# Gate and up products with both halves of the activations in one 512-wide matmul, and the joins of a quad spread over its products

## The chip, the cores and the metric

The kernel runs on one core of one Trainium2 chip. The metric is the device time of one execution in microseconds (us), the median of three runs. The profile is of one further execution. TensorE (PE) multiplies, with its weight loads shown apart as PEld; VectorE (DVE) and ScalarE (ACT) do elementwise work; GpSimd (POOL) and SyncE (SP) here mostly issue DMAs. Each of them takes its instructions in the order of its own program and waits on semaphores for the others.

## The reference, cut to what matters

One encoder layer on 512 tokens of width 2048: a token mixer, a layer norm, and a SwiGLU block with `D_FF = 5632`. The change touches the first half of the last one:

```python
def swiglu(h, w_gate, w_up, w_down):
    return (jax.nn.silu(h @ w_gate) * (h @ w_up)) @ w_down
...
        h = x * (1.0 + sc_f) + sh_f
        y = swiglu(h, w_gate[l], w_up[l], w_down[l])
```

## The kernel before

**Three products for one.** Every fp32 operand is kept as a rounded part `hi` and a remainder `lo = x - hi`, and a product is `hi*hi + lo*hi + hi*lo` with three matmuls (helper `mm3`, lines 241 to 243 when `gu_product` calls it). Weights come by DMA as a `raw` tile of 128x1024; `split` makes `whi` on ACT (L276) and `wlo` on DVE (L277). Activations are the tiles `mhi`, `mlo`.

**Seven products for eight.** Gate and up are computed with a Strassen-like scheme on 2x2 blocks. The work is cut into 44 quads, numbered `n`: even ones are gate, odd ones up, and two that follow each other form a pair `p`. One quad has the seven products p1, q7, r6, p2, q5, q4, p3 (table `SEVEN`), each a contraction over 8 blocks of 128, so 8 x 3 = 24 matmuls, each 256 tokens wide. p1, p2, q5 and p3 multiply the activations themselves (`mhi`, `mlo`), q7, r6 and q4 sums of their blocks (tiles `R7`, `R6`, `R4`, which hold hi in their first 256 columns and lo in the next). Three PSUM banks collect a quad: `V` (p1, r6, q5, p3), `Y` (q7, q4) and `A` (p2).

**Sums of weight blocks.** Four of the seven products need sums of weight blocks: S3 for q7, S1 for q5, S2 for r6, S4 for p3. From the fifth quad on, DVE makes them from the raw blocks (`add_behind`: L1284, L1287, L1290, L1293, each 128x1024). For the first four quads (`NPRE = 4`) they were made earlier by DMAs.

**What sets the order.** One loop walks over all products; a step is one product. In step `s` the program first issues the split of the weights of step `s + 3` (`prepare`, with four `whi`/`wlo` pairs in turn, `NW = 4`), then the DMAs (`fetch_behind`), then the matmuls of the step, then what is done with its PSUM bank (`gu_use`), then the sums of weight blocks (`add_behind`, at steps given by a table of how many steps ahead). No scheduler reorders anything: on each engine the instructions stand in that order. In `gu_use` ACT copies banks out (`e`, `yv`, `vq`) and DVE joins them; a gate quad ends in Silu on ACT, an up quad in multiplications on DVE and in `give`, which makes the operands of the down projection.

The first four quads are interleaved (first all their p1 and p2, then their q7, then r6), while DVE and ACT still finish the layer norm and make R7, R6, R5 and R4 (`finish1`, `block_sums` with `put`).

Of the kernel before, what the change touches and what calls it, by code (L numbers as in the profile page):

```python
# [25 lines left out]
FT = mybir.dt.float32  # L26
# [114 lines left out]
def layer_kernel(ctx, tc, ws, wa, wada, xt, x, cin, bada, lbl, ghg, gcq, gckv, ln1c, lnrow, ident, lvm, dist, out):  # L141
# [955 lines left out]
        W.held["out", 3, i] = hold_out  # L1097


    m_hi, m_lo = [], []  # L1100
    for j in range(KD):
        if j % 4 == 0:
            m_hi.append(big(f"mhi{j // 4}"))
            m_lo.append(big(f"mlo{j // 4}"))
# [4 lines left out]
        split(sa, m_hi[j // 4][:, j % 4], m_lo[j // 4][:, j % 4])  # L1109
# [31 lines left out]
    def finish1(t):  # L1141


        mv1[t] = mv = ln_scale(st1[t], "mv1")
        s = slice(t * P, t * P + P)
        z = zt.pop(t)
        for c in (2, 3, 0, 1):
            if t == NT - 1 and c < 2:
                nc.scalar.activation(z[:, c], z[:, c], AF.Identity, scale=mv[:, 3:4], bias=mv[:, 4:5])
            else:  # L1150
                nc.vector.tensor_scalar(z[:, c], z[:, c], mv[:, 0:1], mv[:, 3:4], op0=OP.subtract, op1=OP.mult)
        raws = first_raws() if t == 0 else None
        if t == NT - 1:
            second.append(passing("h22"))
        for _ in range(1 if t < NT - 1 else 3):
            yield
        for pair in (2, 0):
            bs = []
            for c in (pair, pair + 1):
                ps = bank("zt")  # L1160
                for k in range(4):
                    nc.tensor.transpose(ps[:, k * P:k * P + P], z[:, c, k * P:k * P + P], id_t)
                bs.append((c, ps))
            for c, ps in bs:
                h2 = hraw[t, c] = raws[c] if raws else second[0][:, c - 2] if second and c >= 2 else heap("h2")
                for k in range(4):
                    n = 4 * c + k
                    a, b = h2[:, k * P:k * P + P], ps[:, k * P:k * P + P]
                    nc.scalar.activation(a, b, AF.Identity, scale=colA[:, n:n + 1], bias=colB[:, n:n + 1])
                if t < 2 or c >= 2:  # L1170
                    v = h2.rearrange("p (k q) -> p k q", k=4)
                    nc.vector.tensor_copy(m_hi[c][:, :, s], v)
                    nc.vector.tensor_sub(m_lo[c][:, :, s], v, m_hi[c][:, :, s].bitcast(FT))
            yield

    sums = {}

    def put(v, hi, lo):

        v = v.rearrange("p (k q) -> p k q", k=4)  # L1180
        nc.scalar.activation(hi, v, AF.Copy)
        nc.vector.tensor_sub(lo, v, hi.bitcast(FT))

    def block_sums():


        for i in ("R7", "R6", "R5", "R4"):
            raw = {}
            for t in (0, 1):
                for c in range(2):  # L1190
                    h11, h12, h21, h22 = (hraw.get(at) for at in ((t, c), (t + 2, c), (t, c + 2), (t + 2, c + 2)))
                    if i == "R7":
                        raw[t, c] = h22
                        nc.vector.tensor_sub(h22, h12, h22)
# [12 lines left out]
            if i == "R4":  # L1207
                second.clear()
            if i != "R5":
                sums[i] = [passing(f"{i}_{c}", FR) for c in range(2)]  # L1210
            for t, c in list(raw):
                s = slice(t * P, t * P + P)
                s2 = slice(t * P + 2 * P, t * P + 3 * P)
                if i == "R5":
                    put(raw.pop((t, c)), m_hi[c][:, :, s2], m_lo[c][:, :, s2])
                else:
                    put(raw.pop((t, c)), sums[i][c][:, :, s], sums[i][c][:, :, s2])
                yield

    def mh(k):  # L1220
        return m_hi[k // 4][:, k % 4], m_lo[k // 4][:, k % 4]

    def piece(w, n):

# [29 lines left out]
    for n in range(NPRE, 2 * NP2):  # L1254
        s = NPRE * 7 + (n - NPRE) * 7
        for ahead, what in ((8, "11"), (8, "21"), (6, "22"), (4, "12")):
            fetch.setdefault(s - ahead, []).append((("gu", n), what))
        for ahead, what in ((3, "S3"), (3, "S1"), (2, "S2"), (-2, "S4")):
            adds.setdefault(s - ahead, []).append((("gu", n), what))
    for n, u in enumerate(steps):  # L1260
        if u.group[0] == "dn" or u.group in first:
# [95 lines left out]

    def factor(i, k):

        if i[0] == "p":  # L1360
            c, cols = k // 4 + 2 * (i != "p1"), slice(0, 2 * P) if i != "p3" else slice(2 * P, T)
        elif i == "q5":
            c, cols = k // 4, slice(2 * P, T)
        else:
            s = sums["R" + i[1]][k // 4][:, k % 4]
            return s[:, :2 * P], s[:, 2 * P:]
        return m_hi[c][:, k % 4, cols], m_lo[c][:, k % 4, cols]

# [10 lines left out]
    def gu_product(u):  # L1379
        n = u.group[1]  # L1380
        i, name = u.i, CHAIN[u.i]
        if i in FRESH:
            acc[n, name] = bank(name)
        ps = acc[n, name][:, :H]
        whi, wlo = u.pair
        for k in range(8):
            w = slice(k * P, k * P + P)
            mm3(ps, whi[:, w], wlo[:, w], *factor(i, k), i in FRESH and k == 0, k == 7, f=mmul, skip_group_check=True)
            if n < NPRE and k % 4 == 3:
                side.step()  # L1390

    def gu_use(u):
        n, i = u.group[1], u.i
        p, up = n // 2, n % 2
        ps = acc[n, CHAIN[i]][:, :H]
        t = tmp.setdefault(n, {})
        if i == "p1":
            t["e"] = heap("e")
            nc.scalar.activation(t["e"][:, :H], ps, AF.Copy)
        elif i == "q7":  # L1400
            t["yv"] = heap("yv")
            nc.scalar.activation(t["yv"][:, :H], ps, AF.Copy)
            acc_copy[:] = [t["yv"][:, :1]]
        elif i == "r6":
            nc.scalar.activation(t["yv"][:, H:], ps, AF.Copy)
        elif i == "p2":
            e = t.pop("e")[:, :H]
            if up:
                nc.vector.tensor_add(e, e, ps)
                nc.vector.tensor_mul(act[p][:, :H], act[p][:, :H], e)  # L1410
            else:
                a = act[p] = heap("act")
                nc.vector.tensor_add(a[:, :H], e, ps)
                nc.scalar.activation(a[:, :H], a[:, :H], AF.Silu)
        elif i == "q5":
            vq = heap("vq")[:, :H]
            t["c"] = heap("c") if up else heap("act")
            nc.scalar.activation(vq, ps, AF.Copy)
            acc_copy[:] = [vq[:, :1]]
            nc.vector.tensor_sub(t["c"][:, H:], t["yv"][:, :H], vq)  # L1420
        elif i == "q4":
            c = t.pop("c")
            nc.vector.tensor_sub(c[:, :H], ps, t.pop("yv")[:, H:])
            if up:
                nc.vector.tensor_mul(act[p + NP2], act[p + NP2], c)
            else:
                act[p + NP2] = c
                nc.scalar.activation(c, c, AF.Silu)
        elif up:
            a, b = act.pop(p), act.pop(p + NP2)  # L1430
            nc.vector.tensor_mul(a[:, H:], a[:, H:], ps)
            give(p, a, b)
        else:
            nc.scalar.activation(act[p][:, H:], ps, AF.Silu)
        if i in DONE:
            del acc[n, CHAIN[i]]

    def give(p, a, b):

# [175 lines left out]
    for n, u in enumerate(steps[len(steps) - KEEP:]):  # L1615
        u.place = keep_small if n < 2 else keep_big

    for step in range(len(steps)):
        u = steps[step]
        if step + 3 < len(steps):  # L1620
# [8 lines left out]
        if u.group[0] == "gu":  # L1629
            gu_product(u)  # L1630
            gu_use(u)
        elif not last:
            dn_product(u)
            dn_use(u)
# [9 lines left out]
            nc.gpsimd.tensor_copy(pace, acc_copy[0])  # L1644
            more(1)
        if step == nsteps - 1:
            del m_hi, m_lo
            mh = None
# [144 lines left out]
```

## Time and profile before

| | |
|---|---|
| median of three runs | 2784.64 us (2781.55 to 2786.32) |
| the profiled execution | 2785.46 us, span 2783.5 us |
| instructions in the span | 41852 |
| PE busy | 2748.0 us, 99% of the span |
| PEld, DVE, ACT, POOL busy | 87%, 74%, 42%, 24% |
| mean granted TensorE clock | 0.996 |

The span reaches from the first to the last instruction; the 2 us that the execution is longer lie around it. A share is a mean over the whole span. Matmuls overlap each other, so a busy PE says only that something is in flight; what a matmul takes of PE's time is the distance from its start to the start of the next one.

### The profile page before, as it was taken

What the parts mean: (1) busy time and instruction counts of PE and PEld (TensorE: products, weight loads), DVE (VectorE), ACT (ScalarE), POOL (GpSimd) and SP (SyncE); (2) the same over time, 40 slices, a digit from 0 to 9 for tenths busy, and PEclk for the clock granted to TensorE, in tenths of its full rate; (3) what the DMA queues carried; (4) which work ended last, traced back from release to release, by engine and by line L of the source; (5) the groups of instructions that cost most, each with busy time, mean ns of one, the idle gap of its engine ahead of it and who ended that gap; (6) DMA issues with size and microseconds to landing.
All of it is one profiled execution on the core that took longest, in us unless ns stands there. A gap on an engine that the chain in (4) does not pass through costs nothing.

```text
span 2783.5 us, 41852 instructions
## 1 busy us (share of the span) xinstructions
PE 2748.0 (99%) x16090; PEld 2421.5 (87%) x16090; DVE 2047.7 (74%) x2900; ACT 1158.6 (42%) x1732; POOL 676.3 (24%) x911
## 2 busy tenths in 40 slices
PE   8999999999999999999999999999999999999998
PEld 6778888888888888788888999999999999888886
DVE  7877687878872577545667778777777787885697
ACT  4334434233322455322236444444444444554453
POOL 0011042424000475431210122212221223750000
PEclk9999999999999999999999999999999999999999
DMA  9866545555984897796955556676555768987775
GB/s 381 294 217 209 176 152 176 175 176 184 317 296 144 225 271 239 240 286 191 263 190 168 194 175 193 173 190 186 184 183 178 190 180 246 315 300 239 237 254 178
DMA packets 179274, 609.86 MB, mean 219 GB/s; under 512 B 23201, under 2 KB 23505, under 8 KB 176001
## 3 DMA queue, kind: packets, MB, share of 16 engines
q1 hardware_dynamic: 126866, 430.18, 44.9%
q0 software_dynamic: 51776, 176.44, 23.5%
q8 instruction: 126, 2.06, 0.3%
q14 instruction: 74, 0.61, 0.1%
q10 hardware_dynamic: 432, 0.57, 0.1%
HBM read 564.09 MB, written 149.70 MB: 256 GB/s over the span
## 4 chain that ended last, share of the span: by engine, by line
PE 91%; DVE 3%; DMA 2%; ACT 1%; issue 1%; POOL 1%; SPq 0%; DVEq 0%; ACTq 0%; POOLq 0%
PE gb L233 6%; PE y L233 6%; PE ga L233 6%; PE V L243 6%; PE V L241 6%; PE V L242 6%; PE pb L233 3%; PE g L233 3%; PE dnV L243 3%; PE dnV L242 3%; PE Y L243 3%; PE Y L241 3%; PE dnV L241 3%; PE v L233 3%; PE Y L242 3%; PE pa L233 3%
## 5 line engine op out<-in xcount | busy, mean ns | idle before, releaser
L277 DVE TENSOR_TENSOR wlo<-raw,whi 128x1024 fp32r<-128x1024 f32 x374 | 470.0, 1263 | 248.4 <-ACT whi L276 248.1
L276 ACT ACTIVATE whi<-raw 128x1024 fp32r<-128x1024 f32 x374 | 395.3, 1058 | 329.5 <-PE dnV L243 113.5
L363 DVE TENSOR_TENSOR wlo<-raw,whi 128x1024 fp32r<-128x1024 f32 (+1 forms) x228 | 284.5, 1251 | 111.3 <-ACT whi L351 110.8
L351 ACT ACTIVATE whi<-raw 128x1024 fp32r<-128x1024 f32 (+1 forms) x228 | 233.7, 1038 | 201.2 <-DVE raw L1086 74.3
L243 PE MATMUL V<-mhi,wlo 128*128 128x256 f32 x1056 | 298.6, 283 | 0.0
L241 PE MATMUL V<-mhi,whi 128*128 128x256 f32 x1056 | 298.5, 283 | 0.0
L242 PE MATMUL V<-mlo,whi 128*128 128x256 f32 x1056 | 298.3, 282 | 0.0
L241 PEld LDWEIGHTS V<-mhi,whi 128*128 128x128 f32 x1056 | 202.2, 191 | 0.0
L242 PEld LDWEIGHTS V<-mlo,whi 128*128 128x128 f32 x1056 | 202.2, 191 | 0.0
L243 PEld LDWEIGHTS V<-mhi,wlo 128*128 128x128 f32 x1056 | 202.2, 191 | 0.0
L241 PE MATMUL Y<-R,whi 128*128 128x256 f32 x704 | 196.6, 279 | 2.2 <-ACT whi L276 2.2
L243 PE MATMUL Y<-R,wlo 128*128 128x256 f32 x704 | 196.1, 279 | 1.8 <-DVE wlo L277 1.8
L242 PE MATMUL Y<-R,whi 128*128 128x256 f32 x704 | 196.1, 279 | 0.0
L243 PE MATMUL dnV<-whi,flo 128*128 128x512 f32 x352 | 138.7, 394 | 0.0
L242 PE MATMUL dnV<-wlo,fhi 128*128 128x512 f32 x352 | 138.0, 392 | 0.0
L241 PE MATMUL dnV<-whi,fhi 128*128 128x512 f32 x352 | 136.6, 388 | 0.0
L241 PEld LDWEIGHTS Y<-R,whi 128*128 128x128 f32 x704 | 133.9, 190 | 2.4 <-ACT whi L276 2.4
L243 PEld LDWEIGHTS Y<-R,wlo 128*128 128x128 f32 x704 | 133.6, 190 | 2.2 <-DVE wlo L277 2.2
L242 PEld LDWEIGHTS Y<-R,whi 128*128 128x128 f32 x704 | 133.8, 190 | 0.0
L276 ACT ACTIVATE whi<-wrow 128x1024 fp32r<-128x1024 f32 x80 | 84.4, 1055 | 84.7 <-DVE wrow L1284 84.7
L997 POOL DMA_DIRECT2D sum_dn<-in_ws x132 | 97.1, 811 | 58.5 <-DMA sum_dn<-in_ws 49.3
L233 PE MATMUL ga<-hThi,whi 128*128 128x512 f32 x256 | 101.9, 398 | 0.0
(461 smaller groups left out, 7747.6 us busy)
## 6 DMA issues: line engine op xcount, KB each, us to landing
raw<-in_ws SPq DMA_DIRECT2D x414, 512.0 KB, 5.1
sum_dn<-in_ws POOLq DMA_DIRECT2D x132, 512.0 KB, 8.6
raw<-in_wada SPq DMA_DIRECT2D x128, 512.0 KB, 5.1
raw<-sum_dn SPq DMA_DIRECT2D x88, 512.0 KB, 3.6
rawb<-in_wada SPq DMA_DIRECT2D x22, 1024.0 KB, 12.0
sum_dn<-sum_dn POOLq DMA_DIRECT2D x44, 512.0 KB, 5.1
wrow<-in_ws SPq DMA_DIRECT2D x40, 512.0 KB, 6.7
sum_gu<-in_ws POOLq DMA_DIRECT2D x24, 512.0 KB, 9.3
```

The costliest lines, as they stand in the source:

```text
L233: mmul(*a, **k)
L241: f(ps, ahi, bhi, start=first, stop=False, **k)
L242: f(ps, ahi, blo, start=False, stop=False, **k)
L243: f(ps, alo, bhi, start=False, stop=last, **k)
L276: nc.scalar.activation(hi, src, AF.Copy)
L277: engine.tensor_sub(lo, src, hi.bitcast(FT))
L351: nc.scalar.activation(hi, src, AF.Copy)
L363: nc.vector.tensor_sub(lo, src, hi.bitcast(FT))
L997: nc.gpsimd.dma_start(d_sum[g, dst], block(g, src), **({"accum_op": OP.add} if add else {}))
```

## The change

**The layout.** `mhi` and `mlo` become tiles `m_t` that hold, for each block k of the contraction, the hi row and the lo row next to each other (512 columns each). `R` tiles had both already.

**The matmuls.** `gu_product` takes one matmul of `whi` with hi and lo side by side (512 columns: for `m_t` two runs of 256, for `R` one run of 512), and one of `wlo` with hi (256 columns) that adds to the second half of the bank. A bank now holds two halves, M and X, whose sum is the product. So each k has two matmuls instead of three.

**The joins.** Since a bank has two halves, copies and joins are 512 wide or are followed by an addition of the halves. What was done at q5, q4 and p3 is put off to a generator `gu_join`, whose first part runs after p3 and whose second part runs after p1 of the next quad. Two sums of weight blocks move: S3 from 3 to 4 steps ahead, S4 from 2 steps behind to 1.

```diff
-            mm3(ps, whi[:, w], wlo[:, w], *factor(i, k), i in FRESH and k == 0, k == 7, f=mmul, skip_group_check=True)
+            both, hi = factor(i, k)
+            mmul(wide, whi[:, w], both, start=i in FRESH and k == 0, stop=k == 7, skip_group_check=True)
+            mmul(wide[:, 1], wlo[:, w], hi, start=False, stop=k == 7, skip_group_check=True)
...
-        for ahead, what in ((3, "S3"), (3, "S1"), (2, "S2"), (-2, "S4")):
+        for ahead, what in ((4, "S3"), (3, "S1"), (2, "S2"), (-1, "S4")):
...
+        def whole(v, name):
+
+            if n < NPRE:
+                if "yv" not in t:
+                    t["yv"] = heap("yv")
+                h = t["yv"][:, :H] if name == "y" else t["yv"][:, H:]
+                copy(h, M, AF.Copy)
+                add(h, h, X)
+            else:
+                h = heap(name)
+                copy(h, ps, AF.Copy)
+            t[name] = h
+            acc_copy[:] = [h[:, :1]]
...
         elif i == "p2":
-            e = t.pop("e")[:, :H]
+            e = t.pop("e")
+            add(e, e, ps)
             if up:
-                nc.vector.tensor_add(e, e, ps)
-                nc.vector.tensor_mul(act[p][:, :H], act[p][:, :H], e)
+                add(e[:, :H], e[:, :H], e[:, H:])
+                nc.vector.tensor_mul(act[p][:, :H], act[p][:, :H], e[:, :H])
             else:
                 a = act[p] = heap("act")
-                nc.vector.tensor_add(a[:, :H], e, ps)
-                nc.scalar.activation(a[:, :H], a[:, :H], AF.Silu)
+                add(a[:, :H], e[:, :H], e[:, H:])
+                copy(a[:, :H], a[:, :H], AF.Silu)
...
+            if n < NPRE:
+                sub(c[:, :H], M, v)
+                add(c[:, :H], c[:, :H], X)
             else:
-                act[p + NP2] = c
-                nc.scalar.activation(c, c, AF.Silu)
-        elif up:
+                sub(v, ps, v)
+                add(c[:, :H], v[:, :H], v[:, H:])
+        else:
+            z = t["z"] = heap("z")
+            copy(z, ps, AF.Copy)
...
+    def gu_join(n):
...
+        if n < NPRE:
+            sub(c[:, H:], y, vq[:, :H])
+            sub(c[:, H:], c[:, H:], vq[:, H:])
+        else:
+            sub(y, y, vq)
+            add(c[:, H:], y[:, :H], y[:, H:])
+        if up:
+            nc.vector.tensor_mul(act[p + NP2], act[p + NP2], c)
+        else:
+            act[p + NP2] = c
+            nc.scalar.activation(c, c, AF.Silu)
+        del c, y, vq
+        t.clear()
+        yield
+        if up:
             a, b = act.pop(p), act.pop(p + NP2)
-            nc.vector.tensor_mul(a[:, H:], a[:, H:], ps)
+            add(z[:, :H], z[:, :H], z[:, H:])
+            nc.vector.tensor_mul(a[:, H:], a[:, H:], z[:, :H])
+            del z
             give(p, a, b)
         else:
-            nc.scalar.activation(act[p][:, H:], ps, AF.Silu)
-        if i in DONE:
-            del acc[n, CHAIN[i]]
+            a = act[p][:, H:]
+            add(a, z[:, :H], z[:, H:])
+            nc.scalar.activation(a, a, AF.Silu)
...
             gu_product(u)
             gu_use(u)
+            for _ in joining:
+                break
+            if u.i == "p3":
+                for _ in joining:
+                    pass
+                joining = gu_join(u.group[1])
+                if u.group[1] < NPRE - 1:
+                    for _ in joining:
+                        pass
+                else:
+                    next(joining)
```

What the rounding to hi and lo of an R5 or layer-norm block did with one instruction on 512 columns is now done with two on 256 (`mparts`), since the block's four rows lie in two tiles.

**What DVE does around a gate quad's end, before.** `L1423` joins q4, `L1290` is the sum S2, `L1293` the sum S4, `L1413` the join of p2 of the next quad, and the `wlo` rows are weight splits, up to two of them in one row:

```order
L1423 TENSOR_TENSOR act<-Y,yv 128x256
L1290 TENSOR_TENSOR raw<-raw 128x1024
L277 TENSOR_TENSOR wlo<-raw,whi 128x1024
L277 TENSOR_TENSOR wlo<-wrow,whi 128x1024
L277 TENSOR_TENSOR wlo<-raw,whi 128x1024 x2
L1293 TENSOR_TENSOR raw<-raw,wrow 128x1024
L277 TENSOR_TENSOR wlo<-raw,whi 128x1024
```

The same stretch on DVE after the change: `L1456` and `L1457` join q4, `L1301` is S2, `L1474` and `L1475` the first part of `gu_join`, `L1492` its second part, `L1304` is S4:

```order
L1456 TENSOR_TENSOR v<-Y,v 128x512
L1457 TENSOR_TENSOR act<-v 128x256
L1301 TENSOR_TENSOR raw<-raw 128x1024
L277 TENSOR_TENSOR wlo<-raw,whi 128x1024
L1474 TENSOR_TENSOR y<-y,vq 128x512
L1475 TENSOR_TENSOR act<-y 128x256
L277 TENSOR_TENSOR wlo<-wrow,whi 128x1024
L1492 TENSOR_TENSOR act<-z 128x256
L277 TENSOR_TENSOR wlo<-raw,whi 128x1024
L1304 TENSOR_TENSOR raw<-raw,wrow 128x1024
```

Five joins stand in this stretch where one stood, and two of the splits now come right behind a join.

**What ACT does there, before.** `L1428` is the 512-wide Silu of q4 and q5, `L1434` the Silu of p3 straight from PSUM, `L1399` and `L1402` copy the next quad's p1 and q7:

```order
L1428 ACTIVATE act<-act 128x512
L276 ACTIVATE whi<-raw 128x1024
L1434 ACTIVATE act<-V 128x256
L276 ACTIVATE whi<-wrow 128x1024
L1399 ACTIVATE e<-V 128x256
L276 ACTIVATE whi<-raw 128x1024
L1402 ACTIVATE yv<-Y 128x256
```

After the change `L1460` copies p3, `L1480` is the 512-wide Silu (it reads what `L1475` on DVE writes), `L1493` the Silu of p3 (it reads what `L1492` writes):

```order
L1460 ACTIVATE z<-V 128x512
L1480 ACTIVATE act<-act 128x512
L276 ACTIVATE whi<-wrow 128x1024
L1430 ACTIVATE e<-V 128x512
L1493 ACTIVATE act<-act 128x256
L276 ACTIVATE whi<-raw 128x1024
L1424 ACTIVATE y<-Y 128x512
```

Both Silus moved to a place directly ahead of a `whi` split, and both read a result that DVE has just made.

## Rows read from the trace of the kernel before

**Rows 1.** The page: span, and busy time of each engine with its instructions.
```profile
span 2783.5 us, 41852 instructions
PE 2748.0 (99%) x16090; PEld 2421.5 (87%) x16090; DVE 2047.7 (74%) x2900; ACT 1158.6 (42%) x1732; POOL 676.3 (24%) x911
```

**Rows 2.** What PE waited for in gate/up: us in total, times, longest.
```profile
PE Y L241 <- ACT whi L276: 2.2, 1, 2.2
PE Y L243 <- DVE wlo L277: 1.8, 2, 1.1
```

**Rows 3.** Tile V: ns min/median/max, first and last start in us.
```profile
L241 PE MATMUL V<-mhi,whi x1056: 276/283/283, 1472.2 to 2348.5; 128*128 128x256 f32 x176
...
L241 PE MATMUL V<-R,whi x352: 276/276/276, 1516.9 to 2337.2; 128*128 128x256 f32 x176
```

**Rows 4.** Windows: us, busy PE, PEld, DVE, ACT, POOL (instructions), granted clock, DMA.
```profile
1475.00:1515.00 40.00, 35.13 (x267) 34.08 (x266) 34.29 (x54) 26.60 (x50) 1.09 (x2) 0.91 0.44 142
...
1700.00:2300.00 600.00, 600.00 (x5125) 600.00 (x5124) 472.75 (x531) 278.15 (x385) 134.05 (x227) 1.00 0.63 183
```

**Rows 5.** Timeline of PE: first matmul of four products (start, us, what).
```profile
1702.28 0.29 PE L241 MATMUL Y<-R,whi 128*128 128x256 f32 x1
...
1705.02 0.28 PE L241 MATMUL V<-R,whi 128*128 128x256 f32 x1
...
1707.74 0.28 PE L241 MATMUL A<-mhi,whi 128*128 128x256 f32 x1
...
1710.60 0.28 PE L241 MATMUL V<-mhi,whi 128*128 128x256 f32 x1
```

**Rows 6.** The chain that ended last: two stretches of 512-wide matmuls (start, us).
```profile
1163.40 5.60 PE pa L233 x24
...
1292.27 146.30 PE y L233 x644
```

**Rows 7.** Timeline of PE: 512-wide stream from the pool that holds R.
```profile
1449.14 0.39 PE L233 MATMUL y<-wo,mlo 128*128 128x512 f32 x1
...
1449.84 0.39 PE L233 MATMUL y<-wo,mlo 128*128 128x512 f32 x1
```

**Rows 8.** DVE groups of 1700 to 2300 us: busy, mean ns, idle before them.
```profile
L277 DVE TENSOR_TENSOR wlo<-raw,whi 128x1024 fp32r<-128x1024 f32 x153 | 185.9, 1224 | 109.9 <-ACT whi L276 109.9
...
L1425 DVE TENSOR_TENSOR act<-act,c 128x512 f32<-128x512 f32 x15 | 10.4, 692 | 0.5
L1420 DVE TENSOR_TENSOR c<-yv,vq 128x256 f32<-128x256 f32 x15 | 6.4, 425 | 13.1 <-ACT vq L1418 13.1
```

**Rows 9.** Groups of the whole span: 512-wide DVE and ACT instructions that read PSUM.
```profile
L409 DVE TENSOR_TENSOR early<-early 128x512 f32<-128x512 f32 x24 | 16.0, 683 | 10.0 <-PE early L233 9.9
L933 ACT ACTIVATE pthi<-t 128x512 fp32r<-128x512 f32 x32 | 17.3, 597 | 1.5 <-PE t L931 1.5
```

**Rows 10.** Timeline of DVE in steady gate/up (idle before in brackets).
```profile
1810.40 0.41 DVE L1413 TENSOR_TENSOR act<-e,A 128x256 f32<-128x256 f32 x1
1812.25 1.23 DVE L277 TENSOR_TENSOR wlo<-raw,whi 128x1024 fp32r<-128x1024 f32 x1 [1.43 <-ACT whi L276]
...
1837.20 1.22 DVE L1290 TENSOR_TENSOR raw<-raw 128x1024 f32<-128x1024 f32 x1
1839.62 1.23 DVE L277 TENSOR_TENSOR wlo<-raw,whi 128x1024 fp32r<-128x1024 f32 x1 [1.21 <-ACT whi L276]
```

**Rows 11.** Timeline of ACT: Silu and split behind it, and the 512-wide Silu.
```profile
1810.85 0.42 ACT L1414 ACTIVATE act<-act 128x256 f32<-128x256 f32 x1 [1.62 <-DVE act L1413]
1811.18 1.04 ACT L276 ACTIVATE whi<-raw 128x1024 fp32r<-128x1024 f32 x1
...
1817.79 0.63 ACT L1428 ACTIVATE act<-act 128x512 f32<-128x512 f32 x1 [1.68 <-DVE act L1423]
```

**Rows 12.** Timeline of DVE in the first four quads, weight splits only.
```profile
1507.43 1.23 DVE L277 TENSOR_TENSOR wlo<-raw,whi 128x1024 fp32r<-128x1024 f32 x1 [1.43 <-ACT whi L276]
...
1515.32 1.22 DVE L277 TENSOR_TENSOR wlo<-raw,whi 128x1024 fp32r<-128x1024 f32 x1
...
1523.87 1.23 DVE L277 TENSOR_TENSOR wlo<-raw,whi 128x1024 fp32r<-128x1024 f32 x1 [0.98 <-ACT whi L276]
```

More of the change, by code (lines that the diff above doesn't have):

```diff
@@ L1097, in layer_kernel, with mh, mparts @@
         W.held["out", 3, i] = hold_out
-    m_hi, m_lo = [], []
+    m_t = []
+    def mh(k):
+        return m_t[k // 2][:, 2 * (k % 2)], m_t[k // 2][:, 2 * (k % 2) + 1]
+    def mparts(c, s):
+        for n in range(2):
+            v = m_t[2 * c + n].rearrange("p (k h) q -> p k h q", h=2)
+            yield slice(2 * n, 2 * n + 2), v[:, :, 0, s], v[:, :, 1, s]
     for j in range(KD):
-        if j % 4 == 0:
-            m_hi.append(big(f"mhi{j // 4}"))
-            m_lo.append(big(f"mlo{j // 4}"))
+        if j % 2 == 0:
+            m_t.append(big(f"m{j // 2}"))
         more(2)
@@ L1108, in layer_kernel @@
         nc.vector.tensor_add(sa, sa, sb)
-        split(sa, m_hi[j // 4][:, j % 4], m_lo[j // 4][:, j % 4])
+        split(sa, *mh(j))
         if j + AHEAD < KD:
@@ L1171, in finish1, with put @@
                     v = h2.rearrange("p (k q) -> p k q", k=4)
-                    nc.vector.tensor_copy(m_hi[c][:, :, s], v)
-                    nc.vector.tensor_sub(m_lo[c][:, :, s], v, m_hi[c][:, :, s].bitcast(FT))
+                    for k, hi, lo in mparts(c, s):
+                        nc.vector.tensor_copy(hi, v[:, k])
+                        nc.vector.tensor_sub(lo, v[:, k], hi.bitcast(FT))
             yield
     sums = {}
-    def put(v, hi, lo):
+    def put(v, parts):
         v = v.rearrange("p (k q) -> p k q", k=4)
-        nc.scalar.activation(hi, v, AF.Copy)
-        nc.vector.tensor_sub(lo, v, hi.bitcast(FT))
+        parts = list(parts)
+        for k, hi, lo in parts:
+            nc.scalar.activation(hi, v[:, k], AF.Copy)
+        for k, hi, lo in parts:
+            nc.vector.tensor_sub(lo, v[:, k], hi.bitcast(FT))
     def block_sums():
@@ L1214, in block_sums @@
                 if i == "R5":
-                    put(raw.pop((t, c)), m_hi[c][:, :, s2], m_lo[c][:, :, s2])
+                    put(raw.pop((t, c)), mparts(c, s2))
                 else:
-                    put(raw.pop((t, c)), sums[i][c][:, :, s], sums[i][c][:, :, s2])
+                    put(raw.pop((t, c)), [(slice(0, 4), sums[i][c][:, :, s], sums[i][c][:, :, s2])])
                 yield
-    def mh(k):
-        return m_hi[k // 4][:, k % 4], m_lo[k // 4][:, k % 4]
     def piece(w, n):
@@ L1358, in factor @@
     def factor(i, k):
[L1360 to L1367, printed above, removed]
+        if i[0] == "p" or i == "q5":
+            k += 8 * (i in ("p2", "p3"))
+            cols = slice(0, 2 * P) if i in ("p1", "p2") else slice(2 * P, T)
+            v = m_t[k // 2][:, 2 * (k % 2):2 * (k % 2) + 2, cols]
+            return v, v[:, 0]
+        s = sums["R" + i[1]][k // 4][:, k % 4].rearrange("p (h q) -> p h q", h=2)
+        return s, s[:, 0]
     H = 2 * P
@@ L1383, in gu_product @@
             acc[n, name] = bank(name)
-        ps = acc[n, name][:, :H]
+        ps = acc[n, name]
+        wide = ps.rearrange("p (h q) -> p h q", h=2)
         whi, wlo = u.pair
@@ L1394, in gu_use @@
         p, up = n // 2, n % 2
-        ps = acc[n, CHAIN[i]][:, :H]
+        ps = acc[n, CHAIN[i]]
+        M, X = ps[:, :H], ps[:, H:]
+        copy, add, sub = nc.scalar.activation, nc.vector.tensor_add, nc.vector.tensor_sub
         t = tmp.setdefault(n, {})
+        def whole(v, name):
[10 more added lines that the diff above has]
+            acc_copy[:] = [h[:, :1]]
@@ L1397, in gu_use @@
         if i == "p1":
             t["e"] = heap("e")
-            nc.scalar.activation(t["e"][:, :H], ps, AF.Copy)
+            copy(t["e"], ps, AF.Copy)
         elif i == "q7":
-            t["yv"] = heap("yv")
-            nc.scalar.activation(t["yv"][:, :H], ps, AF.Copy)
-            acc_copy[:] = [t["yv"][:, :1]]
+            whole(ps, "y")
         elif i == "r6":
-            nc.scalar.activation(t["yv"][:, H:], ps, AF.Copy)
+            whole(ps, "v")
         elif i == "p2":
-            e = t.pop("e")[:, :H]
+            e = t.pop("e")
@@ L1415, in gu_use @@
         elif i == "q5":
[L1416 to L1418 removed]
+            vq = t["vq"] = heap("vq")
+            copy(vq, ps, AF.Copy)
             acc_copy[:] = [vq[:, :1]]
[L1420 removed]
         elif i == "q4":
[L1422 to L1425, printed above, removed]
[L1426 to L1429 removed]
+            c = t["c"] = heap("c") if up else heap("act")
@@ new lines, in gu_use @@
+            v = t.pop("v")
+            if n < NPRE:
+                sub(c[:, :H], M, v)
+                add(c[:, :H], c[:, :H], X)
+            else:
+                sub(v, ps, v)
[3 more added lines that the diff above has]
+            copy(z, ps, AF.Copy)
+        if i in DONE:
+            del acc[n, CHAIN[i]]
+    def gu_join(n):
+        p, up = n // 2, n % 2
+        add, sub = nc.vector.tensor_add, nc.vector.tensor_sub
+        t = tmp.pop(n)
+        c, y, vq, z = (t.pop(x) for x in ("c", "y", "vq", "z"))
+        if n < NPRE:
[13 more added lines that the diff above has]
+        if up:
@@ L1616, in layer_kernel @@
         u.place = keep_small if n < 2 else keep_big
+    joining = iter(())
     for step in range(len(steps)):
@@ L1646, in layer_kernel @@
         if step == nsteps - 1:
-            del m_hi, m_lo
-            mh = None
+            for _ in joining:
+                pass
+            m_t = None
             sums.clear()
```

## The prediction, as put on record before the run

> **What bounds the kernel now.** The page comes first: PE is busy for 99% of the span, DVE for 74%, ACT for 42% [rows 1]. The list of waits says the same more sharply: in the whole gate/up part PE waited 4.0 us for its weights, once for ACT and twice for DVE [rows 2]. This part runs from 1472.2 to 2348.5 us [rows 3]. A window inside it, from 1700 to 2300 us, shows PE without a gap at full clock, with 5125 matmuls in 600 us, so 0.1171 us each [rows 4]; DVE is busy for 472.75 us of it (79%) and ACT for 278.15 us (46%). A pair of quads, gate and up, has 2 x 7 x 24 = 336 matmuls, so it takes PE 39.3 us, and DVE has 472.75 / 600 x 39.3 = 31.0 us of work in it. The reader is to see that PE is the bound, but that DVE has only 8.3 us to spare in each pair, and that its groups show what fills them: 109.9 us of idle time before `wlo`, all of it waiting for `whi` from ACT [rows 8].
>
> **What PE gains.** The change takes one matmul in three away, 2464 of 7392, and makes another one twice as wide. The timeline of PE gives the distance between products [rows 5]: 24 matmuls on `R` take 2.72 to 2.74 us, so 0.340 us for a group of three, and 24 on `mhi`/`mlo` take 2.86 us, so 0.358. A single one of 256 is thus 0.113 or 0.119. For 512 columns there are two prices: 0.227 us in the out projection (146.30 / 644) and 0.233 in pa (5.60 / 24) [rows 6]. The tile `wo`, from the pool that also holds `R`, has 0.233 as a moving operand (three matmuls from 1449.14 to 1449.84) [rows 7]. I take 0.233 for `R`: 0.233 + 0.113 = 0.347 instead of 0.340, a loss of 7 us over the 1056 groups of q7, r6 and q4 (at 0.227: none). For `m_t` the 512 columns are two runs of 256, which no row shows; they lie between one run (0.227) and two matmuls (0.238). With 0.119 for the second matmul a group takes 0.346 to 0.357 instead of 0.358; I take the middle, 0.352, a gain of 8 us over 1408 groups (bounds: 16 and 0). So on PE the whole change is worth about -1 us, from -16 to +7: three streams of 256 and one of 512 with one of 256 carry the same columns, and the weight loads were already hidden behind the streams (PE without a gap).
>
> **What DVE and ACT get in exchange.** ACT copies 512 columns (0.60 us [rows 9]) instead of 256 (0.42 for a Silu of that width [rows 11]) four times, and copies p3 as well: some 1.3 us in the 19.7 us of a quad, which takes it from 46% to 53%. Its own time hides that. DVE is another matter. In each quad the join of p2 becomes 512 wide from PSUM (0.683 us [rows 9]) and needs an addition of the halves (0.425 [rows 8]), where it was one of 256 (0.425): +0.68. The join of q4: the same, +0.68. The join of q5 becomes 512 wide (0.692) with an addition: +0.69. p3 gets an addition of its halves: +0.43. That is 2.48 us in a quad and 5.0 in a pair: DVE's work rises from 31.0 to 36.0 us. In itself this still fits into PE's 39.3.
>
> What decides is what DVE waits for while it has work behind it. Two patterns have rows. After the sum S2 comes its split at once: DVE adds until 1838.42, ACT makes `whi`, and `wlo` starts at 1839.62, after 1.21 us of idle time [rows 10]. After the p2 join of a gate quad ACT first does the Silu (0.42) and then the `whi` that stands behind it (1.04) [rows 11], and DVE's next `wlo` waits 1.43 us [rows 10]. In both, work that is ready stands behind the waiting `wlo`.
>
> After the change, by the order of instructions: the first pattern stays (S2, in each quad: 2 x 1.21 = 2.4 us in a pair). The second moves. At p2 the sum S3 (1.22) now lies between, which leaves 0.2 of it. But the first part of `gu_join` in a gate quad is followed on ACT by the 512-wide Silu (0.63 [rows 11]) and the `whi` of the next p2, whose `wlo` is DVE's next instruction: 1.43 + 0.63 - 0.42 = 1.64 us. The second part is followed by the Silu of p3 and the `whi` of S1, with its `wlo` next on DVE: 1.43. S4 loses its wait, since another split now lies between. Sum: 2.4 + 0.2 + 1.64 + 1.43 = 5.7 us in a pair. None of these four waits is for PE, so DVE's being late doesn't shorten them.
>
> The Trainium skill (TensorE: Matmul & The Clock Gate, section on the architecture of the array, queue depths) says that ACT and DVE are strict first-in first-out queues. The trace agrees: 109.9 us of waiting with ready sums behind it. By that rule a pair costs DVE its work plus these waits; if it could pass a waiting `wlo`, PE would set the pace and the first rival below would hold.
>
> So a round of DVE through a pair is 36.0 + 5.7 = 41.7 us, against 39.3 of PE: 2.4 us too long. Weights are split three steps ahead, so DVE can fall behind by up to three products (3 x 2.8 = 8.4 us) before PE stands still. There are 20 pairs from the fifth quad on: 20 x 2.36 = 47 us. DVE enters late (next paragraph), so I count half of the lead as a cushion: 47 - 4 = 43 us. What PE gains or loses by itself drops out, as long as its pair stays under 41.7.
>
> **The first four quads.** Here DVE is already the bound: between the waits before 1507.43 and 1523.87 us no `wlo` waits for ACT any more [rows 12], and the first `wlo` for r6 ends at 1516.54, 0.3 us before that product starts [rows 3, 12]. In front of it DVE gets four p2 joins (4 x 0.68 = 2.7), one q7 addition (0.43), and the splits of R5 and the last norm block in halves (two of 0.425 for one of 0.692, six times, 0.16 each, about 1.0). Sum 4.1, less 0.3: about 4 us later, bounds 2 and 8, the upper one if the longer wait also lowers the clock, which in this stretch fell to 0.91 [rows 4]. Everything ahead (layout of the `m` tiles) and the down projection keep their instructions: 0.
>
> **The sum.** 2785.5 (this execution; the median of the runs is 0.8 lower) + 43 + 4 = 2832 us, 1.7% slower.
>
> **The rivals.**
> PE keeps the pace. If the waits come to less than 39.3 - 36.0 = 3.3 us in a pair (because ACT gets to its Silus earlier than I put them, or DVE's additions overlap more), DVE only eats its idle time. Then the time is 2785.5 + 4 - 1 = 2789, from 2774 (both bounds in PE's favour) to 2796. For it: 8.3 us of idle time in a pair. Against it: of those, the waits counted above don't go away by themselves. The case on the other side lies here: faster, if the two runs of `m_t` stream like one and `R` like the out projection. The same page (section on the back-to-back gap) gives a matmul N/2.4 + 2.5 ns, so 215.8 and 109.2 ns: a group of three would fall from 327.5 to 325.0, 6 us in all, and this rival would come to 2783. The trace has 227 to 233 and 113 to 119 ns for the same widths.
> The clock falls. When PE waited in the first quads, 40 us had a mean clock of 0.91 [rows 4], which is some 7 us at half speed (1.2 instead of 2.4 GHz) and 3.6 us of lost work. If PE's waits of 2.4 us in a pair bring that on in every other pair, it costs up to 36 us, of which the standing still would absorb about a third: 2855.
> DVE's waits are only half as long as counted, 2.9 us in a pair with 37.5 us of work because the additions hang on each other: 40.4, 1.1 too long, 2785.5 + 22 - 4 + 4 = 2808. This is the lower end of my own case; the upper end, with 0.1 us more at ten hand-overs, is 42.7 and 2852.
>
> **How the numbers follow.** DVE and ACT set the pace: 0.75, own range 2808 to 2850. PE keeps it: 0.16 (0.05 of it faster, 0.05 unchanged, 0.06 slower, since 2774 to 2796 straddles 2785). The clock falls as well: 0.09. A measurement of this kernel can tell 0.2%, 5.6 us, from no change. Faster 0.06, same 0.06, slower 0.88. The range 2798 to 2855 leaves out most of the second case and the top of the third.
>
> **What would show it.** In the profile after: PE waits for `wlo` (L277) all through gate/up, 40 us or more in sum; DVE about 86% busy in the steady part, with its idle time before `wlo` behind L1301, L1475 and L1492; a pair of about 41.5 us; PE's matmuls still 0.227 to 0.238 and 0.113 to 0.119 apart where they don't wait; ACT above 50%. I am wrong if DVE's groups show under 3.3 us of idle time in a pair, or if PE has no gaps.

## Result and profile after

The changed kernel takes 2835.07 us (median of 4 runs, 2832.78 to 2836.36); the kernel before, beside it, 2784.4. Ratio 1.0179, 95% interval 1.0167 to 1.0191: 1.8% slower. The profiled execution has a span of 2834.6 us, 51.1 more than before.

The page, its span and the busy time of each engine, against [rows 1]:

```profile
span 2834.6 us, 37231 instructions
PE 2764.9 (98%) x13626; PEld 2316.4 (82%) x13626; DVE 2151.8 (76%) x3112; ACT 1210.5 (43%) x1780; POOL 682.5 (24%) x911
```

Tile V, first and last start, against [rows 3]:

```profile
L1401 PE MATMUL V<-m,whi x1056: 388/398/469, 1469.7 to 2400.0; 128*128 128x512 f32 x176
...
L1401 PE MATMUL V<-R,whi x352: 389/397/629, 1516.7 to 2388.7; 128*128 128x512 f32 x176
```

These two rows say where the 51.1 us lie. Gate/up starts 2.5 us earlier (1469.7 against 1472.2; no cause was looked for). From there to the first product r6 it takes 47.0 us instead of 44.7: +2.3. From r6 to the last product on `m` it takes 883.3 instead of 831.6: +51.7. What follows is 0.4 shorter. So nearly the whole loss lies behind that first r6; that it comes evenly, pair by pair, is shown by the starts of r6 below.

What PE waited for most in gate/up (us in total, times, longest), against [rows 2]:

```profile
PE V L1401 <- ACT e L1430: 35.3, 20, 2.2
```

Twenty waits, one for each pair of quads from the fifth quad on, and not for a `wlo` but for a copy of ACT, `e`. All waits of PE in gate/up together are 42.0 us. A window (columns as in [rows 4]) shows the steady part:

```profile
1700.00:2300.00 600.00, 574.58 (x3199) 495.75 (x3198) 509.06 (x615) 292.04 (x384) 129.12 (x212) 0.99 0.56 174
```

A pair has 224 matmuls now, so 600 x 224 / 3199 = 42.0 us, against 39.3. DVE is busy for 85% (35.6 us of a pair), ACT for 49%. The timeline of PE shows one pair after another at the product r6 (start, us, what, idle time ahead):

```profile
1672.50 0.50 PE L1401 MATMUL V<-R,whi 128*128 128x512 f32 x1 [2.11 <-ACT e L1430]
...
1798.50 0.50 PE L1401 MATMUL V<-R,whi 128*128 128x512 f32 x1 [2.11 <-ACT e L1430]
...
1840.40 0.50 PE L1401 MATMUL V<-R,whi 128*128 128x512 f32 x1 [2.21 <-ACT e L1430]
...
1841.93 0.63 PE L1401 MATMUL V<-R,whi 128*128 128x512 f32 x1
...
1882.56 0.50 PE L1401 MATMUL V<-R,whi 128*128 128x512 f32 x1 [0.98 <-ACT e L1430]
...
2386.11 0.50 PE L1401 MATMUL V<-R,whi 128*128 128x512 f32 x1 [2.11 <-ACT e L1430]
```

From the first to the last of these are 17 pairs: 713.61 / 17 = 41.98 us each. The row of 1841.93 lies in a stretch at half clock, and the next wait is shorter by 1.2 us (0.98), while the distance between the two r6 grows by only 0.26 (42.16, against 41.90 from 1798.50 to 1840.40). Twelve of the 17 pairs take 41.9 us, five with such a stretch 42.2. So PE has little to do with the length of a round. Who has, the chain of waits tells, here ahead of 1840.40 (start, us, what):

```profile
1833.62 1.15 DVE raw L1301
...
1834.88 1.07 ACT whi L276
...
1835.97 1.23 DVE wlo L277
...
1837.83 0.44 DVE act L1475
...
1838.83 1.04 ACT whi L276
1839.87 0.49 ACT e L1430
...
1840.40 0.50 PE V L1401
```

DVE and ACT alternate, and PE comes last. The timeline of DVE shows the same place with its idle times, and that of ACT the queue behind the Silu:

```profile
1833.54 1.22 DVE L1301 TENSOR_TENSOR raw<-raw 128x1024 f32<-128x1024 f32 x1
1835.97 1.23 DVE L277 TENSOR_TENSOR wlo<-raw,whi 128x1024 fp32r<-128x1024 f32 x1 [1.21 <-ACT whi L276]
...
1837.83 0.43 DVE L1475 TENSOR_TENSOR act<-y 128x256 f32<-128x256 f32 x1
1839.90 1.23 DVE L277 TENSOR_TENSOR wlo<-wrow,whi 128x1024 fp32r<-128x1024 f32 x1 [1.64 <-ACT whi L276]
1841.04 0.42 DVE L1492 TENSOR_TENSOR act<-z 128x256 f32<-128x256 f32 x1
1842.89 1.23 DVE L277 TENSOR_TENSOR wlo<-raw,whi 128x1024 fp32r<-128x1024 f32 x1 [1.43 <-ACT whi L276]
```

```profile
1838.29 0.63 ACT L1480 ACTIVATE act<-act 128x512 f32<-128x512 f32 x1 [1.87 <-DVE act L1475]
...
1839.77 0.58 ACT L1430 ACTIVATE e<-V 128x512 f32<-128x512 f32 x1
```

The copy `e` takes p1 out of the bank V, to which r6 then adds, so r6 must wait for it. It stands on ACT behind the 512-wide Silu and a `whi` (1838.83 in the chain), and that Silu waits for DVE (1.87 us). In sum over 1700 to 2300 us, the groups of DVE (busy, mean ns, idle before), against [rows 8]:

```profile
L277 DVE TENSOR_TENSOR wlo<-raw,whi 128x1024 fp32r<-128x1024 f32 x143 | 174.8, 1223 | 61.5 <-ACT whi L276 60.0
L277 DVE TENSOR_TENSOR wlo<-wrow,whi 128x1024 fp32r<-128x1024 f32 x57 | 69.5, 1219 | 23.0 <-ACT whi L276 23.0
```

84.5 us in 14.3 pairs: 5.9 us of waiting in each, and 35.6 + 5.9 = 41.5; the other 0.5 are short gaps of DVE before other instructions.

### The profile page after: what moved, and what is told of

Read it like the earlier page. It is cut to its first block, busy times and chain, and to the rows that moved or that the text cites. A ratio compares the mean times of both kernels' runs of the same rounds, so it can differ in the third digit from the quotient of the medians.

```text
span 2834.6 us, 37231 instructions
## 1 busy us (share of the span) xinstructions
PE 2764.9 (98%) x13626; PEld 2316.4 (82%) x13626; DVE 2151.8 (76%) x3112; ACT 1210.5 (43%) x1780; POOL 682.5 (24%) x911
## 4 chain that ended last, share of the span: by engine, by line
PE 64%; DVE 19%; issue 7%; ACT 6%; DMA 3%; POOL 1%; SPq 0%; ACTq 0%; DVEq 0%; POOLq 0%
PE gb L233 6%; PE y L233 6%; PE ga L233 6%; DVE wlo L277 6%; ACT whi L276 5%; PE g L233 3%; PE dnV L241 3%; PE dnV L243 3%; PE dnV L242 3%; PE v L233 3%; PE pb L233 3%; PE early L233 2%; PE qb L233 2%; PE V L1401 2%; PE pa L233 2%
## 5 line engine op out<-in xcount | busy, mean ns | idle before, releaser
L1401 PE MATMUL V<-m,whi 128*128 128x512 f32 x1056 | 376.9, 399 | 0.0
L1402 PE MATMUL V<-m,wlo 128*128 128x256 f32 x1056 | 296.2, 280 | 0.0
L1401 PE MATMUL Y<-R,whi 128*128 128x512 f32 x704 | 253.9, 399 | 3.2 <-ACT whi L276 3.2
L1401 PEld LDWEIGHTS V<-m,whi 128*128 128x128 f32 x1056 | 198.3, 188 | 49.7
L1402 PE MATMUL Y<-R,wlo 128*128 128x256 f32 x704 | 198.8, 282 | 1.4 <-DVE wlo L277 1.4
L1402 PEld LDWEIGHTS V<-m,wlo 128*128 128x128 f32 x1056 | 199.5, 189 | 0.0
L1401 PE MATMUL V<-R,whi 128*128 128x512 f32 x352 | 134.3, 418 | 35.3 <-ACT e L1430 35.3
L1401 PEld LDWEIGHTS Y<-R,whi 128*128 128x128 f32 x704 | 133.6, 190 | 35.7 <-ACT whi L276 3.9
L233 PE MATMUL y<-whi,m 128*128 128x512 f32 x448 | 139.0, 390 | 0.0
L1402 PEld LDWEIGHTS Y<-R,wlo 128*128 128x128 f32 x704 | 133.4, 189 | 2.2 <-DVE wlo L277 2.2
L1401 PE MATMUL A<-m,whi 128*128 128x512 f32 x352 | 127.0, 400 | 0.0
L277 DVE TENSOR_TENSOR wlo<-wrow,whi 128x1024 fp32r<-128x1024 f32 x80 | 97.6, 1219 | 32.9 <-ACT whi L276 32.9
L1401 PEld LDWEIGHTS V<-R,whi 128*128 128x128 f32 x352 | 68.9, 196 | 57.9 <-ACT e L1430 41.7
```

Of the source, the lines that this page charges most:

```text
L233: mmul(*a, **k)
L277: engine.tensor_sub(lo, src, hi.bitcast(FT))
L1401: mmul(wide, whi[:, w], both, start=i in FRESH and k == 0, stop=k == 7, skip_group_check=True)
L1402: mmul(wide[:, 1], wlo[:, w], hi, start=False, stop=k == 7, skip_group_check=True)
```

## Experiments

Theory A is that of the prediction: DVE's work and its waits for ACT make a round of 41.9 us, longer than PE's. Its rivals: B, PE itself stands in the circle, through `e`; C, the new matmuls cost the time. Each run is compared with runs of the kernel before on the same chip (2783.2 to 2783.4). The changed kernel was not run again there; differences from it are taken from its 2835.07, which stood beside 2784.4. The pair in a text below is 600 us by the matmuls of a pair (224, 336 or 272) over the number in the window from 1700 to 2300 us.

**One wait taken away at the head of the circle (silu512_late).**

```diff
             act[p + NP2] = c
-            nc.scalar.activation(c, c, AF.Silu)
         del c, y, vq
         t.clear()
         yield
+        if not up:
+            nc.scalar.activation(act[p + NP2], act[p + NP2], AF.Silu)
```

> The changed kernel, with the 512-wide Silu of a gate quad issued one product later, so that ACT's queue has the next weight rounding and the copy of p1 ahead of it. Theory A (DVE and ACT go round in 41.9 us per pair of quads, PE needs 39.5; every wait of DVE for whi has its own price): the wait of 1.64 us behind L1475 goes, 20 pairs, so -33 us: 2802, from 2796 to 2808, and the other waits (1.21 twice, 1.43) stay as they are. Theory B (PE itself stands in the circle: its wait is for ACT's copy e, L1430, which stood behind this Silu and is now ahead of it): PE's waits vanish altogether and the time falls to PE's own pace, 2786 to 2790. Theory C (the new matmuls are what costs the time): no change, 2835.

Measured: 2798.67 us, ratio 1.0052 (1.0037 to 1.0067), 36 us less than the changed kernel. Its wait of PE, its window, and DVE's group of the splits out of `wrow`:

```profile
PE V L1401 <- ACT vq L1447: 8.3, 16, 0.5
```

```profile
1700.00:2300.00 600.00, 592.76 (x3353) 512.44 (x3352) 530.36 (x644) 303.90 (x403) 147.26 (x224) 1.00 0.58 179
```

```profile
L277 DVE TENSOR_TENSOR wlo<-wrow,whi 128x1024 fp32r<-128x1024 f32 x60 | 73.2, 1219 | 0.0
```

The wait of 1.64 us is gone, a pair takes 40.1 us, and PE, which no longer waits for `e`, now waits for another copy, `vq`. Under B nothing would have been left to wait for. A holds.

**One wait at its tail (siluz_late).** The Silu of the last join, one product later:

```diff
             add(a, z[:, :H], z[:, H:])
+            del z
+            yield
             nc.scalar.activation(a, a, AF.Silu)
```

> The changed kernel, with the 256-wide Silu of a gate quad's last join (behind L1492) issued one product later, nothing else. Theory A (a DVE and ACT round of 41.9 us per pair, each wait with its own price): the wait of 1.43 us goes, 20 pairs, -29 us: 2806, from 2801 to 2812. Theory B (PE in the circle, through the copy e behind the 512-wide Silu, which stays where it is ahead of that copy): 2829 to 2835.

Measured: 2810.96 us, ratio 1.0103 (1.0087 to 1.0118), 24 us less. Its wait of PE, its window, and on DVE the split that had waited 1.43 us:

```profile
PE V L1401 <- ACT e L1430: 18.2, 20, 0.9
```

```profile
1700.00:2300.00 600.00, 585.82 (x3305) 505.86 (x3304) 524.22 (x637) 303.29 (x400) 132.50 (x219) 1.00 0.57 176
```

```profile
1834.16 1.22 DVE L277 TENSOR_TENSOR wlo<-raw,whi 128x1024 fp32r<-128x1024 f32 x1 [0.23 <-ACT whi L276]
```

0.23 us of the wait remain, so 1.20 x 20 = 24 us are gained and not 29. B is refuted: order and length of what stands ahead of `e` are unchanged, and PE's wait for it is half as long.

**The waits behind S2 (s2_early).** `(2, "S2")` becomes `(3, "S2")` in the list of sums.

> The changed kernel, with the sum S2 made one product earlier, behind S1, so that its rounding on ACT lies a product ahead of its wlo on DVE. Theory A (DVE and ACT round of 41.9 us per pair): two waits of 1.21 us per pair go, 2.4 us, which leaves 39.5, PE's own pace: 2786 to 2794. Theory B (PE waits for the copy e behind the 512-wide Silu, which this edit does not touch): the wait of 1.8 us per pair stays, 2825 to 2835. Theory C (matmuls): 2835.

Measured: 2786.58 us, ratio 1.001 (1.000 to 1.0019), 48 us less. Its window, and the starts of three products:

```profile
1700.00:2300.00 600.00, 600.00 (x3404) 520.96 (x3403) 537.39 (x651) 316.47 (x412) 139.87 (x225) 1.00 0.59 181
```

```profile
1704.54 0.40 PE L1401 MATMUL V<-R,whi 128*128 128x512 f32 x1
...
1707.36 0.39 PE L1401 MATMUL A<-m,whi 128*128 128x512 f32 x1
...
1710.18 0.40 PE L1401 MATMUL V<-m,whi 128*128 128x512 f32 x1
```

PE has no gap any more, DVE does the same work in less time, and a pair is 39.48 us. Here PE's own price of the change can be read: 2.82 us for a product on R (0.352 a group, 0.340 before) and 2.82 on `m` (0.353, 0.358 before). By 48 and 64 groups that is 39.5 us in a pair against 39.3: +3 us in all.

**All three (all_waits).**

> The changed kernel with the three edits together: S2 one product earlier, the 512-wide and the last 256-wide Silu one product later. Theory A: the round falls by 2.4 + 1.64 + 1.43 to 36.4 us, below PE's 39.5, so nothing is gained beyond the kernel with S2 alone: 2787, from 2783 to 2790, no gaps of PE, DVE idle where it was waiting for PE. If the rounds were not what set the time, or the waits cost more than they were counted, it falls below 2780.

Measured: 2785.87 us, ratio 1.0008 (0.9999 to 1.0017), no different from s2_early. With PE as the bound, less waiting on DVE brings nothing more, as A has it.

**The matmuls put back (three_narrow).**

```diff
-            mmul(wide, whi[:, w], both, ...)
+            st = i in FRESH and k == 0
+            mmul(wide[:, 0], whi[:, w], both[:, 0], start=st, ...)
+            mmul(wide[:, 1], whi[:, w], both[:, 1], start=st, ...)
```

> The changed kernel, with each 512-wide matmul of gate/up taken apart into two of 256 that write the two halves of the same bank: three matmuls of 256 as before the change, but sums and joins as after it. Theories A and B (the joins and their waits cost the time): unchanged, 2835, from 2831 to 2839; matmul starts 113 to 120 ns apart, PE waits as long as in the changed kernel plus what its own pace saves. Theory C (the 512-wide or two-run matmuls cost the time): back to 2785 to 2795.

Measured: 2839.32 us, ratio 1.0201 (1.0186 to 1.0216). Two sums are started in one bank here, and the values that come out are not those of the reference, so it serves for its time alone; kind, number and order of the instructions are as described. It lies 0.3 us above the range that A and B gave. Its wait and its window:

```profile
PE V L1402 <- ACT e L1432: 34.3, 20, 2.1
```

```profile
1700.00:2300.00 600.00, 576.37 (x4817) 572.75 (x4816) 509.01 (x614) 292.81 (x385) 130.07 (x215) 0.99 0.57 175
```

A pair is 41.9 us with the old matmul widths and the new joins: C is refuted.

**More work on DVE, in the kernel after (extra_add) and in the one before (before_extra).**

```diff
+            if n >= NPRE:
+                spare = heap("spare")
+                add(spare[:, :H], t["y"][:, :H], t["y"][:, :H])
+                del spare
```

In the kernel before, the addition stands at the same step and reads `act` in place of `y`.

> The changed kernel, with one more addition of 128x256 on DVE at the p3 step of the quads from the fifth on, ahead of the join, into a tile that nobody reads (the output does not change). Theory A (DVE and ACT set the pace): each adds its 0.42 us to the round, 40 quads, +17 us: 2852, from 2847 to 2857. Theory C (PE sets the pace, DVE has room at 76% busy): 2835. Theory B: the addition of a gate quad delays the 512-wide Silu and with it the copy e, that of an up quad does not: +8 us, 2843.

> The kernel before, with the same extra addition of 128x256 on DVE at the p3 step of the quads from the fifth on, into a tile that nobody reads. Theory A: DVE's round in the kernel before is below PE's 39.3 us per pair (31.0 us of work), so the addition is free: 2784, within 4 us. Rival (DVE's work shows in the time anyway, because each addition delays a wlo): +17 to +21 us, 2803.

Measured: after the change 2858.5 us (ratio 1.0267, 1.0251 to 1.0282), 23 us more; before it 2783.54 (1.0002, 0.9993 to 1.0011), no difference. The windows of extra_add and of before_extra:

```profile
1700.00:2300.00 600.00, 566.57 (x3117) 488.11 (x3116) 507.29 (x624) 287.61 (x377) 124.91 (x206) 0.97 0.55 169
```

```profile
1700.00:2300.00 600.00, 600.00 (x5125) 600.00 (x5125) 481.39 (x565) 277.62 (x383) 137.02 (x227) 1.00 0.62 183
```

An addition of the same size is free in one kernel (5125 matmuls in the window with it and without it) and is paid in full in the other. The price was put too low, and 2858.5 lies above the range given: a pair grew by 1.14 us on average (600 x 224 / 3117 = 43.12). Where the clock had not fallen, two r6 are 42.96 apart, against 41.90: 0.53 for an addition, not 0.42. The rest of the 1.14 comes with the clock (0.97 in the window): a pair behind a stretch at half clock takes 43.2, as in the changed kernel some 0.27 more, and there are more of them here. Two r6 of extra_add, with full clock between them:

```profile
1803.89 0.50 PE L1401 MATMUL V<-R,whi 128*128 128x512 f32 x1 [2.05 <-ACT e L1430]
...
1846.85 0.50 PE L1401 MATMUL V<-R,whi 128*128 128x512 f32 x1 [2.73 <-ACT e L1430]
```

On DVE's timeline the next instruction starts 0.52 behind the start of the extra one:

```profile
1821.76 0.42 DVE L1463 TENSOR_TENSOR spare<-y 128x256 f32<-128x256 f32 x1
1822.28 0.69 DVE L1478 TENSOR_TENSOR y<-y,vq 128x512 f32<-128x512 f32 x1
```

**A kernel that takes what pays (mixed_all).** The three edits of order, and the products on R as three matmuls of 256 again, with joins to match (not shown).

```diff
+            if i[0] == "p" or i == "q5":
                 mmul(wide, whi[:, w], both, ...)
                 mmul(wide[:, 1], wlo[:, w], hi, ...)
+            else:
+                mm3(wide[:, 0], whi[:, w], wlo[:, w], hi, both[:, 1], ...)
```

> The kernel with the three edits together, and in it the products on R (q7, r6, q4) as three matmuls of 256 into the first half of the bank, as before the change; those on the m tiles (p1, p2, q5, p3) stay as one of 512 and one of 256. Y gets by with 256 columns, and q4 and q7 need no join of halves. By the starts of matmuls in the changed kernel a group on R takes 0.352 us (0.234 + 0.118) and in the kernel before 0.340; a group on m 0.353 against 0.358. If PE sets the pace once DVE and ACT keep up, a pair takes 39.5 - 48 x 0.012 = 38.9 us, 22 pairs: -13 us against the kernel with S2 alone: 2774, from 2768 to 2780, faster than before by 0.3%. If something else holds PE (a transfer, DVE after all), 2783 to 2790.

Measured: 2767.52 us, ratio 0.9945 (0.9933 to 0.9958), faster than both kernels. Its window, and the starts of three products:

```profile
1700.00:2300.00 600.00, 600.00 (x4239) 558.80 (x4239) 537.75 (x671) 317.77 (x421) 146.28 (x233) 1.00 0.64 187
```

```profile
1700.61 0.28 PE L241 MATMUL V<-R,whi 128*128 128x256 f32 x1
...
1703.33 0.39 PE L1402 MATMUL A<-m,whi 128*128 128x512 f32 x1
...
1706.11 0.39 PE L1402 MATMUL V<-m,whi 128*128 128x512 f32 x1
```

R is back at 0.340 (2.72 / 8). A group on `m` fell from 0.353 to 0.347 as well (2.78 / 8), which nobody had expected, and which is worth 64 x 0.0055 x 22 = 8 us, more than what the time lies below the forecast (6.5). Why is open.

**Where the price of a matmul comes from (before_even, wide_even, mixed_even, before_m64).** Two prices for one width had left PE's term uncertain. Three kernels got unused bytes ahead of their pools. In the fourth, before_m64 (its edit is not shown), `mhi` and `mlo` alone were shifted against the multiples of 128 bytes, while all big tiles became 128 bytes longer.

```diff
+    pad_l = lp.tile([P, 24], FT, name="pad_l")
+    pad_r = rp.tile([P, 24], FT, name="pad_r")
```

> The kernel before, with 96 unused bytes per partition ahead of the weight pool and at the outer end of the right side, nothing else: so all big, weight, heap and R tiles begin at a multiple of 128 bytes; before, the big and weight tiles began 32 and the heap and R tiles 96 bytes behind one. Question: are the two prices of a 256-wide matmul (0.113 on R, 0.120 on the m tiles) and of a 512-wide one (0.227 and 0.233) prices of the place? Theory P (yes): a group of three on the m tiles comes down from 0.358 to R's 0.340 or below, 64 groups in 22 pairs, -25 us or more: 2759 or lower. Theory Q (the price belongs to what is multiplied, not to where it lies): 2784, from 2780 to 2788. The Trainium skill (TensorE: Matmul & The Clock Gate, section on the back-to-back gap) gives N/2.4 + 2.5 ns, 109.2 and 215.8; if that were reached here, the estimate by it is about 2640.

> The changed kernel with the three edits of order (S2 earlier, two Silus later) and the same unused bytes, so that its tiles too begin at multiples of 128 bytes. Theory P: a group of 512 and 256 falls from 0.353 to 0.340 or below, 112 groups in 22 pairs, -32 us or more against the same kernel without the bytes: 2755 or lower; if PE's pair then comes below DVE's round (36.4 us), DVE is the bound again. Theory Q: 2786. In both the comparison with the kernel before with the same bytes tells what the wide matmuls are worth by themselves: by columns, the same.

> The mixed kernel (R as three of 256, m as 512 and 256, three edits of order) with the same unused bytes. Theory P: m groups from 0.347 to 0.340 or below, 64 in 22 pairs, -10 us or more: 2758 or lower. Theory Q: 2767.5, from 2764 to 2771.

> The kernel before, with the eight big tiles 128 bytes longer and the activations mhi and mlo of gate/up placed 64 bytes into theirs, so that they begin 96 bytes behind a multiple of 128 like R, while the weight tiles stay at 32. Nothing else moves off its place in the grid of 128 bytes. With all tiles at 0 a matmul of 256 took 0.120 us on R too, where it had taken 0.113. Theory P (the place of the streamed tile, by itself or against that of the weights, sets the price): a group of three on the m tiles falls from 0.358 to R's 0.340, 64 groups in 22 pairs, -25 us: 2758, from 2753 to 2764, if DVE keeps up with a pair of 38.1 us. Theory Q (the m tiles are dearer for another reason, for instance the pool or the layout of their writers): 2784.

Measured: before_even 2793.98 us (ratio 1.0038, 1.0023 to 1.0053), wide_even 2775.47 (0.9961, 0.9943 to 0.998; its runs spread from 2758.76 to 2779.14), mixed_even 2785.39 (1.0005, 0.9996 to 1.0015), before_m64 2783.66 (1.0012, 0.9997 to 1.0027; two of its twelve runs took 2800.66 and 2802.52). Two products of before_even:

```profile
1701.39 0.28 PE L245 MATMUL V<-R,whi 128*128 128x256 f32 x1
...
1704.27 0.28 PE L245 MATMUL A<-mhi,whi 128*128 128x256 f32 x1
```

And of before_m64, the first product on `m`, and one on R with the one on `m` behind it and the next:

```profile
L243 PE MATMUL V<-mhi,whi x1056: 276/280/284, 1482.6 to 2346.8; 128*128 128x256 f32 x176
```

```profile
1712.53 0.28 PE L243 MATMUL V<-R,whi 128*128 128x256 f32 x1
...
1715.25 0.28 PE L243 MATMUL A<-mhi,whi 128*128 128x256 f32 x1
...
1718.03 0.28 PE L243 MATMUL V<-mhi,whi 128*128 128x256 f32 x1
```

Both theories failed. Q fell with before_even, where a product on R costs 2.88 us instead of 2.72 with nothing changed but the places of tiles. But P gave the wrong sign there, and in before_m64 a product on `m` fell only to 2.78, not to R's 2.72; gate/up from the first start on `m` to the last became 12 us shorter (864.2 against 876.3), while it began 10 us later (1482.6), because the stages ahead, whose tiles the longer pitch had moved too, took longer. So the places of the operands change what a matmul costs, by 2 to 6%, but their distance from a multiple of 128 bytes doesn't say how. That stays open.

The windows of before_even and wide_even say more than their times, in which other stages have a part:

```profile
1700.00:2300.00 600.00, 600.00 (x5002) 600.00 (x5002) 462.20 (x523) 270.84 (x370) 126.93 (x225) 1.00 0.62 181
```

```profile
1700.00:2300.00 600.00, 600.00 (x3398) 520.30 (x3397) 542.31 (x652) 315.60 (x409) 135.59 (x228) 1.00 0.62 184
```

With the unused bytes a pair of the kernel before takes 40.3 us instead of 39.3, and a pair with the wide matmuls 39.5, as without the bytes. There a group of three takes 0.360 on every product and one of 512 and 256 takes 0.353. So in these places the wide matmul pays everywhere, once the order is mended (from the first start on `m` to the last 884.6 us against 896.5, the whole 2775.47 against 2793.98), and mixed_even, which gives it up on R, lies between them. Whether the change pays on PE depends on where the tiles lie.

## Why the prediction was right

**The round of DVE and ACT** was its step that mattered, and it held: 36.0 us of work and 5.7 of waits were put down, 35.6 and 5.9 were measured, at the places named (1.21 behind L1301, 1.64 behind L1475, 1.43 behind L1492). Each wait that was taken away gave back about what it had been priced at: 24, 36 and 48 us for 29, 33 and 48 (at the last, PE's own pace had become the bound). The waits are those of queues that go strictly in order, as the Trainium skill says (TensorE: Matmul & The Clock Gate, the architecture section); s2_early shows it best, where DVE only gets the same sum at another place in its queue and 48 us go.

**The sizes** of the terms were further off than the sum. For the quads behind the fourth 43 us were forecast, 51.7 measured. The pair is 41.98 us and not 41.7, with 0.4 less of work, 0.2 more of waits, and 0.5 of DVE's short gaps, which were not counted: +5.6 over 20 pairs. And the cushion of 4 us was hardly there: 20 x 2.64 = 52.8, of which 51.7 arrived. It was half of the lead that the splits have, but PE waited for `e`, a copy without such a lead: 0.24 us at the first of the 20 pairs and 2.20 already at the second. In exchange the first four quads lost 2.3 us instead of 4 and gate/up began 2.5 us earlier. These errors partly cancel, and that is luck: 2832 was forecast, 2835.07 measured.

**PE's own term** was right in kind: about nothing, +3 us where -1 was said (bounds -16 and +7). The group on `m` has the middle that was taken (0.353 for 0.352); that on R was dearer (0.352 for 0.347), since the matmul of 256 behind one of 512 takes more than 0.113 (0.118 in s2_early). All this holds for the places that the tiles have here: the runs with unused bytes show that other places can turn the sign of a term of this size. The first rival, PE keeping the pace at 2789, is what s2_early is, at 2786.6. The Trainium skill's rule for the gap (TensorE: Matmul & The Clock Gate, section on the back-to-back gap) makes an estimate of 0.325 for a group of 512 and 256, for matmuls one by one; these runs disagree, the shortest group of that form being 0.347 (mixed_all).

**The clock** fell as the second rival said, behind five of the fourteen waits of over 2 us, but it cost next to nothing: PE, late from half speed, waited less at the next r6, and 0.26 us were left in each of the five pairs, 1.3 in all.

**Wrong in detail:** PE waits for `e` (35.3 us), not 40 us or more for `wlo`. The prediction followed DVE's queue to its end and not ACT's: the 512-wide Silu holds up a `whi`, and behind it a copy that the bank of r6 needs. ACT reached 49% and not over 50%.

## What to carry to other kernels

An engine with a fifth of its time idle can still become the bound, if in its queue ready work stands behind an instruction that waits for another engine: add up work and waits for one round and compare that with the round of the engine that now sets the pace. Where it does become the bound, look first for a sum or an activation that can be issued one step earlier or later; here one number in a list was worth 48 us, and with the order mended the wide matmul paid only where its group was really shorter, which in turn depended on the places of the tiles. The instruction for which the slowest engine waits need not be the cause; here it was the chain behind it.

## What the hardware showed that was not expected

One matmul shape had several prices in these runs: 256 columns from 0.113 (R before) to 0.120 us (R in before_even, with nothing changed but the places of tiles). After the wait of 2.21 us at 1840.40 PE's granted clock was 0.50 from 1842 to 1845 us, 1.2 instead of 2.4 GHz, and a group took 0.64 us for 0.35; of the thirteen other waits of over 2 us four were followed by such a stretch, and nine were not. The window shows it:

```profile
1842.00:1845.00 3.00, 3.00 (x11) 2.52 (x11) 2.11 (x2) 2.55 (x4) 1.43 (x2) 0.50 0.00 0
```
